# A hybrid state-space and attention block on one core: units moved in the schedule, GELU in place, tied queue order and a token-major end

## The chip, the core and the metric

The kernel runs on one NeuronCore of a Trainium2 chip. The metric is the device time of one execution in microseconds, the median of several runs. The engines are TensorE (PE, whose weight loads are listed apart as PEld), VectorE (DVE), ScalarE (ACT) and GpSimd (POOL); SyncE (SP) issues most of the transfers. Each works through its own queue in order and waits for the others through semaphores.

## The reference

One layer is computed in float32 for 2048 tokens of width 1024:

```
h      = rmsnorm(x);  proj = h @ w_in            # u (512), q, k, v (512 each)
y_ssm  = complex diagonal state-space scan of u (32 groups of 16, 64 states each) + d*u
y_ssm  = gelu(y_ssm);  y_ssm *= sigmoid(y_ssm @ w_glu + b_glu)
y_att  = attention, 8 heads of 64, chunks of 64 frames that see themselves and 8 chunks back,
         with a learned bias by clipped relative distance
x      = x + [rmsnorm(y_ssm), rmsnorm(y_att)] @ w_out
x      = x + (silu(h2 @ w_gate) * (h2 @ w_up)) @ w_down      # h2 = rmsnorm(x), width 2816
out    = rmsnorm(x)
```

## The kernel before

Most products are made three times over: each operand is split into a high part (a cast on ACT) and the rest (a subtraction on DVE), `split` at L151, and `mm3` at L145 issues high by high, high by low and low by high. The kernel is built with a scheduler that puts each engine's instructions in order by priority (about that of the program text) and by its own estimate of when they are ready; it may therefore put an instruction ahead of one that the text has first. PE's instructions of the stages spoken of here are kept in the order of the text.

The work runs in stages. The first 127 us make u and the constants of the state-space part. Then comes the attention stage, `att_phase` (L694), from about 127 to 703 us: 128 steps (four blocks of 512 tokens, four pairs of heads, two heads, four query tiles of 128), and in each step `scores` (one PSUM buffer `sc`, added to the bias and reduced to its least value by DVE at L881, then the exponential on ACT at L884), `transp` for the step two before (five transposes into one PSUM buffer `pt`, copied out by ACT at L899 and by DVE at L900), every fourth step `pv_head`, and then the units.

A unit (`Unit`, L672) is a generator with a first and a last step; `advance(s)` draws so many of its parts that it ends in time. Units are the projections of queries and keys (`qk_unit`, L761) and of values (`v_unit`, L814) at the steps of `CUT`, the scaled and split inputs of the next block (`hT_unit`, L731) at `HTA` and `HTS`, and the eight pairs of `ssm_front` (L568, a product on PE, then a scan of some 100 small operations on POOL) and `ssm_back` (L643, two products for each group, whose result is written to the scratch tensor y). `SX` and `SY` (L669, L670) are their first steps: fronts at 4, 24, 35, 48 and so on to 100, backs at 20, 36 and so on to 114. The second front loads its input into a tile U that the first back still uses. A unit's `pre` says how many steps ahead its loads are issued, all on SP's one queue.

At step 119 (`OPEN`) the generator `mix_phase` (L1001) is opened. Its first `MIX_N` = 26 parts run beside the last steps: y comes in (`fetch`), the weights of the gate (GLU) are split, a GELU of 128x2048 is made for the first 512 tokens (`load`, L1055), eight empty parts (`PY`), the 16 parts of the first block's gate (`glu`, L1078), then `load` for the second block. After the attention stage the second gate, the split of `w_out` and the normed inputs `m` follow (to about 731 us), then the products with `w_out`, gate and up (to about 1782 us) and `down_phase` (L1514). Its last part takes 1024 tokens in pieces of 512, 256 and 256 (`TAIL`): eight tiles of 128 features each, transposed (features on the partitions), the squares summed by products with ones, the root by 14 DVE operations (`newton`, L98), spread over the partitions by transposes (`spread`, `rstd_steps`, L126), multiplied and written out in eight transfers.

Of the kernel before, what the change touches and what calls it, by code (L numbers as in the profile page):

```python
# [9 lines left out]
F32 = mybir.dt.float32  # L10
# [25 lines left out]
OPEN, GSTART = 119, 122  # L36
R1 = 13
SGB = 2
RA1, RA2 = 2, 12
# [3 lines left out]
HTP = 2  # L43
PRO = 0, 0, 2, 2, 2, 2, 0, 0, 0
# [10 lines left out]
TAIL = (0, 512), (512, 256), (768, 256)  # L55
# [26 lines left out]
class K:  # L82
    def __init__(self, tc, io):
        self.tc, self.nc, self.io = tc, tc.nc, io
        self.n = 0
        self.te = Ordered(tc)
        self.ta = self.te if PINA else tc.nc.tensor
# [25 lines left out]

def tok_sums(k, te, ps, c, sq):

    for i in range(4):
        te.matmul(ps[:, c + i : c + i + 1], sq[:, i * P : (i + 1) * P], k.ones[:], start=True, stop=True)
# [8 lines left out]
def rstd_steps(k, te, psum, pool, tag, sq, n, out, nt=None, **kw):  # L126
# [4 lines left out]
    for i in range(nt):  # L131
        for m, sq in enumerate(sqs):
            te.matmul(ps[:, i : i + 1], sq[:, i * P : (i + 1) * P], k.ones[:], start=m == 0, stop=m == len(sqs) - 1)
    with k.tc.high_priority():
        o = newton(k, pool, ps[:, :nt], n, nt)
# [432 lines left out]
def ssm_front(k, p, psum, S, b, eng):  # L568
# [8 lines left out]
    U = S["rsn"][:, : GB * NC].rearrange("p (g c) -> p g c", g=GB) if b and b % 2 == 0 else k.t(p, "U", [P, GB, NC])[:]  # L577
    k.U[b] = U
    load(U.rearrange("p g t -> p (g t)"), S["u"].rearrange("j (c g) n t -> (j c) (g n t)", c=CH)[:, GB * NC * b : GB * NC * (b + 1)])
# [5 lines left out]
    for q in range(GP):  # L585
        ps = k.t(psum, "pj", [P, 2, NC], bufs=2)
        for g2 in range(2):
            k.ta.matmul(ps[:, g2, :], bst[:, 2 * q + g2, :], U[:, 2 * q + g2, :], start=True, stop=True)
# [54 lines left out]
def ssm_back(k, p, psum, S, b):  # L643
# [4 lines left out]
    nc.sync.dma_start(tm[:], S["tm"][:, gs])  # L648
    vm = k.t(p, "Vm", [P, GB, P])
# [18 lines left out]
SX = 4, 24, 35, 48, 61, 74, 87, 100  # L668
SY = 20, 36, 49, 62, 75, 88, 101, 114  # L669


class Unit:  # L672


    def __init__(self, gen, n, s0, s1, pre=0, done=0, light=1, mid=None):
# [3 lines left out]
    def advance(self, s):  # L679
# [3 lines left out]
        want = 1 if self.mid is None or s < self.s0 - self.mid else 2  # L683
# [10 lines left out]
def att_phase(k, ident, S, aw, x0, roots):  # L694

    tc, nc, io, pfs = k.tc, k.nc, k.io, k.pfs
    with ExitStack() as cx:
        hT, vts, qk, keep = {0: tuple(zip(*x0))}, {}, {}, {}

# [5 lines left out]
        def load_ws(sb, ns):  # L705
# [4 lines left out]
            for i, n in enumerate(ns):  # L710
# [5 lines left out]
                elif raws:  # L716
                    with tc.high_priority(offset=-WAY):
# [13 lines left out]
        def hT_unit(sb, q0=0, q1=KT):  # L731
# [13 lines left out]
            else:  # L745
                load(q0)
                for q in range(q0 + 1, q1, 2):
                    load(q, 2)
            for q in range(q0, q1):
# [3 lines left out]
                xt = xts[q]  # L753
                for v, n in zip(hT[sb], ("hi", "lo")):
                    v.append(k.t(aw, f"{n}{q}x" if q < DB and sb % 2 else f"{n}{q}", [P, SB], F32R)[:])
                nc.vector.scalar_tensor_tensor(xt, xt, k.gm[:, q : q + 1], S["rsn"][:, ts], op0=ALU.mult, op1=ALU.mult)
                nc.scalar.copy(hi[q], xt)
                nc.vector.tensor_tensor(lo[q], xt, f32(hi[q]), op=ALU.subtract)
            yield

        def qk_unit(sb, pr):  # L761
# [13 lines left out]
            for c in range(2):  # L775
                if c == 0 or not both:
                    cc = range(2) if both else (c,)
                    pss += [k.t(pfs, "pf", [P, 512]) for _ in cc]
                    for q in range(KT):
                        cs = slice(q * P, (q + 1) * P)  # L780
                        for m in cc:
                            wh, wl = ws[m]
                            mm3(k.ta, pss[m][:], wh[:, cs], wl[:, cs], hi[q], lo[q], q == 0, q == KT - 1)
                            if q == 2:
                                keep_w(4 * m + pr)
                        if q < KT - 1:
                            yield
                ps = pss[c]
                if sb == 0:
                    t = k.t(aa, "yt", [P, SB]) if pr else k.t(aw, "xt", [P, SB], bufs=XB)  # L790
                    nc.vector.tensor_tensor(t[:], ps[:], S["rsn"][:, :SB], op=ALU.mult)
                    ps = t
                for hh in range(2):
                    q2h, q2l, k2 = ts[hh]
                    a = slice(hh * 64, hh * 64 + 64)
                    o = slice(64 - hh * 64, 128 - hh * 64)
                    if c == 0:
                        ways = (a, o) if both and hh == 0 else (a,)
                        for w in ways:
                            nc.scalar.activation(q2h[w, :], ps[a, :], AF.Copy, scale=-0.125)  # L800
                            nc.vector.scalar_tensor_tensor(q2l[w, :], ps[a, :], -0.125, f32(q2h[a, :]), op0=ALU.mult, op1=ALU.subtract)
                        if len(ways) == 1:
                            nc.sync.dma_start(f32(q2h[o, :]), f32(q2h[a, :]))
                            nc.sync.dma_start(f32(q2l[o, :]), f32(q2l[a, :]))
                    else:
                        nc.scalar.copy(k2[a, -SB:], ps[a, :])
                        nc.vector.tensor_tensor(k2[o, -SB:], ps[a, :], f32(k2[a, -SB:]), op=ALU.subtract)
                        if sb < NSB - 1:
                            nc.sync.dma_start(S["k"][sb % 2, 2 * pr + hh], f32(k2[:, -SB:]))
# [4 lines left out]
        def v_unit(sb, fh):  # L814
# [5 lines left out]
            for i in range(4):  # L820
# [15 lines left out]
                if sb == 0:  # L836
                    r = roots()[:, i : i + 1]
                    nc.scalar.activation(vt[:, :, :HD], pv3, AF.Copy, scale=r)
                    nc.vector.scalar_tensor_tensor(vt[:, :, HD:], pv3, r, f32(vt[:, :, :HD]), op0=ALU.mult, op1=ALU.subtract)
                else:  # L840
                    nc.scalar.copy(vt[:, :, :HD], pv3)
                    nc.vector.tensor_tensor(vt[:, :, HD:], pv3, f32(vt[:, :, :HD]), op=ALU.subtract)
# [12 lines left out]
        def scores(st):  # L855
# [25 lines left out]
            nc.vector.tensor_tensor_reduce(  # L881
# [865 lines left out]
```

## Time and profile before

| | |
|---|---|
| median of three runs | 2242.87 us (2241.45 to 2247.27) |
| the profiled execution | 2241.38 us, of which the span in the trace is 2239.6 us |
| mean granted TensorE clock | 0.988 |
| busy PE, DVE, ACT, POOL | 2153.6, 1543.1, 1004.6, 354.1 us |
| bytes moved | 430.16 MB, 192 GB/s on average |

The profile is of one execution. A line of a view names the kernel's line, the engine, the operation and the tiles (written <- read); a bracket at the end of a timeline row gives the idle time of the engine just before it and what ended that. In a view of windows each engine has its busy time in the stretch, and PEclk is the clock that PE was granted (1.00 is full speed).

### The profile page before, as it was taken

To read this page: it belongs to the slowest core of one execution; us is meant where nothing else is said; L and a number is where in the kernel's file an instruction comes from. 1 tells how busy PE (TensorE), PEld (TensorE's weight loads), DVE (VectorE), ACT (ScalarE), POOL (GpSimd) and SP (SyncE) were. 2 spreads that over 40 slices of the span, in tenths; PEclk is the share of its full clock that TensorE was granted. 3 is DMA by queue.
4 is the path that set the end of the run, shared out by engine and by line. 5 is a ranking of instruction groups with operands and counts; after the bars stand their busy time and mean duration, and the time that the engine had idled before them with its cause. 6 is when DMAs were issued, how large, how long until landed. Compare 5 with 4: busy or idle time off the path is not lost.

```text
span 2239.6 us, 30165 instructions
## 1 busy us (share of the span) xinstructions
PE 2153.6 (96%) x10632; PEld 1819.1 (81%) x10632; DVE 1543.1 (69%) x2706; ACT 1004.6 (45%) x1667; POOL 354.1 (16%) x830
## 2 busy tenths in 40 slices
PE   8988898999988999999999999999999999999997
PEld 6777797999977788788888887888888788888886
DVE  8756767555557666767766768767665577688776
ACT  6355565556567541443333335333333343353322
POOL 3354666666600000000000000000000100000000
PEclk9999999999999999999999999999999999999999
DMA  9778867666552436835645557546333495465642
GB/s 330 231 249 283 270 207 229 193 196 193 179 175 99 137 116 206 275 118 173 198 153 200 198 191 258 199 160 207 108 115 97 136 371 198 159 226 183 217 174 76
DMA packets 194664, 430.16 MB, mean 192 GB/s; under 512 B 19792, under 2 KB 38272, under 8 KB 187408
## 3 DMA queue, kind: packets, MB, share of 16 engines
q1 hardware_dynamic: 186768, 403.26, 54.3%
q0 software_dynamic: 7744, 24.97, 3.6%
q8 instruction: 83, 1.36, 0.3%
q14 instruction: 69, 0.57, 0.1%
HBM read 288.95 MB, written 131.10 MB: 188 GB/s over the span
## 4 chain that ended last, share of the span: by engine, by line
PE 81%; DMA 7%; DVE 6%; ACT 2%; issue 2%; SPq 1%; DVEq 0%; ACTq 0%
PE X L76 20%; PE ps L76 18%; PE pf L76 11%; PE Y L76 10%; PE big L76 7%; PE W L76 5%; PE pj L76 4%; PE pt L79 2%; PE sc L76 2%; DMA acc<-x 1%; DMA hd<-wc 1%; DMA x<-xt 1%; DMA lo<-hc 1%; DMA w<-wss 1%; DVE ptl L900 0%
## 5 line engine op out<-in xcount | busy, mean ns | idle before, releaser
L76 PE MATMUL X<-hi,c 128*128 128x512 f32 x1408 | 450.9, 391 | 6.5 <-DVE c L153 3.4
L76 PE MATMUL ps<-hd,hd 128*128 128x512 f32 (+1 forms) x1968 | 428.1, 379 | 3.3 <-DVE hd L153 2.0
L76 PEld LDWEIGHTS ps<-hd,hd 128*128 128x128 f32 x1968 | 356.4, 188 | 73.6 <-DVE hd L153 2.7
L76 PEld LDWEIGHTS X<-hi,c 128*128 128x128 f32 x1408 | 264.9, 188 | 63.6 <-DVE c L153 4.5
L76 PE MATMUL X<-lo,c 128*128 128x512 f32 x704 | 274.7, 390 | 0.0
L153 ACT CAST hd<-hd 128x1536 fp32r<-128x1536 f32 (+1 forms) x106 | 147.5, 1394 | 231.0 <-DMA hd<-hq 174.6
L76 PE MATMUL Y<-hi,c 128*128 128x512 f32 x704 | 225.2, 390 | 2.4 <-DVE u L1428 2.4
L153 DVE TENSOR_TENSOR hd<-hd 128x1536 fp32r<-128x1536 f32 (+1 forms) x106 | 174.1, 1644 | 38.6 <-ACT hd L153 38.3
L1532 POOL DMA_DIRECT2D hd<-hq x7 | 5.3, 757 | 1165.3 <-PE X L76 1151.2
L153 DVE TENSOR_TENSOR c<-S,c 128x512 fp32r<-128x512 f32 x176 | 120.9, 688 | 99.3 <-ACT c L153 99.0
L1424 ACT COPY u<-X 128x512 f32<-128x512 f32 x132 | 77.5, 588 | 197.4 <-PE X L76 197.3
L153 ACT CAST c<-S 128x512 fp32r<-128x512 f32 x176 | 109.4, 622 | 120.8 <-PE Y L76 61.8
L76 PE MATMUL big<-m,woh 128*128 128x512 f32 x512 | 161.5, 397 | 0.0
L76 PEld LDWEIGHTS Y<-hi,c 128*128 128x128 f32 x704 | 132.6, 188 | 31.0 <-DVE u L1428 3.2
L1566 DVE TENSOR_TENSOR acc<-acc,ps 128x512 f32<-128x512 f32 x196 | 130.1, 682 | 37.9 <-PE ps L76 37.7
L76 PEld LDWEIGHTS X<-lo,c 128*128 128x128 f32 x704 | 132.7, 188 | 27.4
L153 ACT CAST c<-raw 128x512 fp32r<-128x512 f32 x132 | 82.2, 623 | 150.2 <-PE Y L76 73.0
L76 PE MATMUL pf<-hi,w 128*128 128x512 f32 x416 | 148.7, 409 | 0.0
L76 PE MATMUL Y<-lo,c 128*128 128x512 f32 x352 | 137.2, 390 | 0.0
L900 DVE TENSOR_TENSOR ptl<-pt,pth 128x640 fp32r<-128x640 f32 (+3 forms) x152 | 98.3, 647 | 54.6 <-ACT pth L899 53.1
L884 ACT ACTIVATE s<-s,mn 128x640 f32<-128x640 f32 (+4 forms) x128 | 97.9, 765 | 61.9 <-DVE mn L881 58.6
L899 ACT CAST pth<-pt 128x640 fp32r<-128x640 f32 (+3 forms) x152 | 83.7, 551 | 83.2 <-PE pt L79 78.8
(451 smaller groups left out, 4269.1 us busy)
## 6 DMA issues: line engine op xcount, KB each, us to landing
w<-wss SPq DMA_DIRECT2D x36, 1024.0 KB, 6.2
hq<-g SPq DMA_DIRECT2D x140, 256.0 KB, 2.1
hd<-hq SPq DMA_DIRECT2D x35, 768.0 KB, 4.4
hd<-wc SPq DMA_DIRECT2D x35, 768.0 KB, 5.8
raw<-in_w_gate SPq DMA_DIRECT2D x44, 512.0 KB, 3.7
raw<-in_w_up SPq DMA_DIRECT2D x44, 512.0 KB, 4.1
wc<-px SPq DMA_DIRECT2D x66, 256.0 KB, 3.1
wss<-w SPq DMA_DIRECT2D x12, 1024.0 KB, 6.1
```

Source lines behind the costliest of these rows:

```text
L76: return self.tc.keep_in_program_order(self.tc.nc.tensor.matmul(*a, **b))
L79: return self.tc.keep_in_program_order(self.tc.nc.tensor.transpose(*a, **b))
L153: return nc.scalar.copy(hi, raw), nc.vector.tensor_tensor(lo, raw, f32(hi), op=ALU.subtract)
L884: nc.scalar.activation(s[:, :nk], s[:, :nk], AF.Exp, bias=mn[:], scale=-1.0, accum_out=sums[sb, pr][:, hh, qp : qp + 1])
L899: nc.scalar.copy(pth[:, a:b, qp, :], pt[:, a:b, :])
L900: nc.vector.tensor_tensor(ptl[:, a:b, qp, :], pt[:, a:b, :], f32(pth[:, a:b, qp, :]), op=ALU.subtract)
L1424: nc.scalar.copy(u[:], ps[:])
L1532: (nc.gpsimd if aside else nc.sync).dma_start(f32(lo), src.rearrange("g p c -> p g c"))
L1566: V.tensor_tensor(a, a, ps[:], op=ALU.add)
```

## The change

It has five parts.

1. **State-space units sooner.** `SX` and `SY` become 4, 19, 33, 45, 56, 68, 80, 92 and 20, 34, 46, 57, 69, 81, 93, 105. The second front (b == 1) loads its input in two halves into the tiles hi0x and lo0x, which the first pair of heads has left, and the second back loads it again into U. All loads but the first front's come four steps ahead.
2. **Inputs of a block.** For the third and fourth block the units of `hT_unit` move from 12 to 6 steps ahead of the block to 26 to 8 ahead; the last five tiles are scaled first and split all at step -9. In the last pair of each block the keys' product takes tiles 3 to 7 first. The value weights of the first block (units 9 and 11) are loaded six steps ahead, not four, and split in two parts.
3. **Order on DVE.** `k.least` is the latest reduction of `scores`. Instructions under `behind()` get an edge that keeps them after it on DVE: the copies out of PSUM of queries, keys and values, the scaling, the splits named above and the gate's splits.
4. **GELU.** At step 108 (`FETCH`) the state-space pool is given back, and y of the first 1024 tokens and half of the gate's weights are loaded. GELU runs in place in four pieces of 128x1024 at steps 111, 113, 115, 117, pinned in ACT's order. `take` then only rearranges each block, eight copies of 128x512 on POOL. `GSTART` is 120 (was 122), and `MIX_N` 21 parts.
5. **The end.** `TAIL` keeps (0, 512) and (512, 256). The last 256 tokens are made token-major (`by_tokens`): tokens on the partitions, 512 features in a PSUM bank, the residual added by products with the identity, the squares summed by ACT's accumulator, the root from ACT's Sqrt and four DVE operations (`root`, `refine`), and the gain taken from a row that one transfer spreads over the partitions. They go to an output of their own, out_t. The sums of the two pieces before use `root` as well.

```diff
-OPEN, GSTART = 119, 122
+FETCH, GELU, OPEN, GSTART = 108, (111, 113, 115, 117), 119, 120
...
-RA1, RA2 = 2, 12
+RA0, RA1, RA2 = 3, 10, 14
...
+HTE, HTM, HTL = (-26, -20), -10, (-9, -8)
...
+def root(k, pool, ps, n, w):
...
+    k.nc.scalar.activation(o[:], ps, AF.Sqrt, scale=1.0 / n, bias=k.eps)
+    V.tensor_scalar(v[:], ps, -0.5 / n, -0.5 * EPS, op0=ALU.mult, op1=ALU.add)
+    return refine(V, v, f, y, o)
...
+    V.reciprocal(y[:], o[:])
+    V.tensor_tensor(f[:], y[:], y[:], op=ALU.mult)
+    V.tensor_tensor(f[:], f[:], v[:], op=ALU.mult)
+    V.scalar_tensor_tensor(o[:], f[:], 1.5, y[:], op0=ALU.add, op1=ALU.mult)
...
+    if b == 1:
+        us = [lent(q).rearrange("p (g c) -> p g c", g=2) for q in range(GP)]
+        for q in range(GP):
+            load(us[q], ssm_input(S, b, slice(q, q + 1)))
...
+    if b == 1:
+        k.U[b] = k.t(p, "U", [P, GB, NC])[:]
+        nc.sync.dma_start(k.U[b], ssm_input(S, b))
...
-SX = 4, 24, 35, 48, 61, 74, 87, 100
-SY = 20, 36, 49, 62, 75, 88, 101, 114
+SX = 4, 19, 33, 45, 56, 68, 80, 92
+SY = 20, 34, 46, 57, 69, 81, 93, 105
...
+        def behind(on=True):
+            return tc.issue_after(k.least) if on and k.least else nullcontext()
...
-                    with tc.high_priority(offset=-WAY):
+                    if n == 11:
+                        yield
+                    with tc.high_priority(offset=-WAY), behind(ns == (9, 11)):
...
+            ahead = q0 and sb > 1
+            if ahead:
+                for q in range(q0, q1):
+                    yield
+                    scaled(q)
...
+                with behind(ahead):
+                    nc.vector.tensor_tensor(lo[q], xts[q], f32(hi[q]), op=ALU.subtract)
...
+                    qs = [*range(DB, KT), *range(DB)] if c and pr == 3 else range(KT)
...
+                with behind():
+                    for hh in range(2):
...
+            k.least = ins.ins
...
+            if s == FETCH:
+                sp.release()
+                k.my0 = tc.alloc_tile_pool(name="my0", reuse_waits="tile", bufs=1)
+                k.y0 = k.t(k.my0, "y0", [P, 4, L, 128])
+                for f in range(4):
+                    nc.sync.dma_start(k.y0[:, f], S["y"][:, f * P : (f + 1) * P, :128].rearrange("j p t -> p j t"))
+                k.wg = k.t(k.my0, "wg", [P, 2, DS])
+                nc.sync.dma_start(k.wg[:], io["w_glu"][: 2 * P].rearrange("(q p) n -> p q n", p=P))
...
+                    if s in GELU:
+                        y = k.y0[:, GELU.index(s)]
+                        tc.keep_in_program_order(nc.scalar.activation(y, y, AF.Gelu_apprx_tanh))
...
+                if sb < 2:
+                    nc.gpsimd.tensor_copy(yo, yv[:, f].rearrange("p j c -> p c j"))
...
+        def by_tokens(t0, hs, ds, acc):
...
+            for c in range(2):
+                for n, ((hh, hl), (dh, dl)) in enumerate(zip(hs, ds)):
+                    mm3(te, ps[c][:], hh[:, 0, ts], hl[:, 0, ts], dh[:, 0, c * 512 : c * 512 + 512], dl[:, 0, c * 512 : c * 512 + 512], n == 0, n == len(hs) - 1, skip_group_check=True)
+                    if n == 0:
+                        for i in range(4):
+                            te.matmul(ps[c][:, i * P : (i + 1) * P], acc[4 * c + i][:, ts], k.ident[:], start=False, stop=False, skip_group_check=True)
...
+                    nc.scalar.activation(j[:], ps[c][:], AF.Square, accum_out=sq[c][:])
...
+                nc.scalar.activation(o[:], sq[1][:], AF.Sqrt, scale=1.0 / D, bias=f[:])
+                V.tensor_scalar(v[:], sq[1][:], -0.5 / D, y[:], op0=ALU.mult, op1=ALU.add)
+                refine(V, v, f, y, o)
+                nc.scalar.activation(ta, ta, AF.Copy, scale=o[:])
+                V.scalar_tensor_tensor(b[:], ps[1][:], o[:], g[:, 512:], op0=ALU.mult, op1=ALU.mult)
...
+        for n, _ in enumerate(chain.from_iterable(by_tokens(t0, hs, ds, acc) for t0 in TOKENS)):
+            if n == 2:
+                last.sums(root=root)
+            if n == 5:
+                last.products()
```

249 lines of the change are left out of this document (153 added, 96 removed).

## The prediction

> **What bounds the kernel now.** The first part of the page comes first, then the stretches of the span, the list of who waited for whom, and the timelines of the places found.
>
> ```profile
> span 2239.6 us, 30165 instructions
> ...
> PE 2153.6 (96%) x10632; PEld 1819.1 (81%) x10632; DVE 1543.1 (69%) x2706; ACT 1004.6 (45%) x1667; POOL 354.1 (16%) x830
> ```
>
> PE is busy 96% of the span, so 2239.6 - 2153.6 = 86 us of idle PE is all there is to win, unless PE's work itself becomes less or faster. Gate, up and down, where most of the time lies, keep PE full and are not touched. The question is which of the idle places the change reaches. Waits of PE in the attention stage, from 120 to 260 us and from 260 to 400 us (total, count, longest), and from 640 to 735 us:
>
> ```profile
> PE sc L76 <- DVE mn L881: 5.7, 1, 5.7
> PE pj L76 <- DMA Bst<-bsts: 2.6, 1, 2.6
> PE sc L76 <- issue: 2.2, 1, 2.2
> ...
> PE pt L79 <- DVE ptl L900: 4.5, 2, 3.1
> PE sc L76 <- DVE k L807: 4.1, 1, 4.1
> ...
> PE pt L79 <- DVE ptl L900: 14.1, 3, 6.6
> ```
>
> An idle PE also costs afterwards. These windows lie right behind the longer waits:
>
> ```profile
> 183.00:188.40 5.40, 4.97 (x23) 5.00 (x24) 1.56 (x7) 1.72 (x6) 4.77 (x14) 0.50 1.01 379
> 370.00:372.60 2.60, 2.60 (x10) 2.36 (x11) 2.13 (x4) 1.16 (x3) 2.50 (x4) 0.50 0.45 183
> 668.70:671.10 2.40, 2.37 (x9) 1.96 (x9) 2.40 (x5) 2.40 (x6) 0.00 (x0) 0.50 0.93 298
> 676.80:681.20 4.40, 4.35 (x15) 3.58 (x15) 0.00 (x0) 4.39 (x2) 0.00 (x0) 0.60 0.00 0
> ```
>
> PE is granted half the clock there (0.50, third number from the end), so busy time times the missing share of the clock is lost as well: 4.97 x 0.50 = 2.5, then 1.3, 1.2 and 4.35 x 0.40 = 1.7 us.
>
> **The attention stage.** Step 12 waits 5.7 us, and 2.5 us go by the clock. The chain of waits and DVE's timeline say for what:
>
> ```profile
> 175.32 4.51 DMA nbb<-nbs
> ...
> 180.53 2.54 DVE L153 TENSOR_TENSOR w<-raw,w 128x512 fp32r<-128x512 f32 x4
> ```
>
> The bias nbb was issued behind the value weights and landed at 179.8; then four splits of these weights (2.54 us) ran ahead of the step's reduction. The weights are now loaded two steps sooner and the splits held behind a reduction. The splits leave the path, the bias lands a little earlier, and the clock stays up if the wait is short: 5 us, between 0 and 8.2.
>
> The second front's loads stood on SP behind the first back's store; with the input in other tiles, loaded at step 15 and not 22, the 2.6 us for Bst go. Moved along are two input loads and Bst (step 15) and a second load of U (512 KB, step 28), behind which SP's small loads have two steps of slack. The 2.2 us before step 24 are keys copied out just before use, whose steps stay. Gain 2.6, between 0 and 4.8. The later fronts and backs move 2 to 9 steps; their products move from one full stretch of PE to another, which costs nothing, and POOL's 354.1 us are at most 44 for each of eight fronts, which stand 11 to 15 steps of some 4 us apart, so a back seldom waits for its scan.
>
> Steps 35 and 56 wait because inputs of a later block were put ahead of copies that PE needs:
>
> ```profile
> 271.14 2.14 DVE L756 SCALAR_TENSOR_TENSOR raw<-raw,g_mix,rsn 128x512 f32<-128x512 f32 x1
> ...
> 362.96 0.82 DVE L881 CUSTOM_DVE_ANT_0 s<-sc,nbb 128x640 f32<-128x640 f32 x1
> ...
> 363.71 0.70 DVE L758 TENSOR_TENSOR lo<-raw,hi 128x512 fp32r<-128x512 f32 x1
> ...
> 366.17 2.99 DVE L758 TENSOR_TENSOR lo<-raw,hi 128x512 fp32r<-128x512 f32 x2
> ```
>
> The scaling is now held behind the step's reduction and the block's inputs come earlier. I take 2.5 of the 3.1 us at step 35 (0 to 3.1). At step 56 and shortly behind it 4.1 + 1.4 us of waiting (4.5 - 3.1 leaves 1.4) and 1.3 us of clock are at stake, but five tiles are split at once in step 55: 5 x 0.70 = 3.5 us of DVE may again stand before a reduction. I take 3.5 of 6.8 (0 to 6.8), and 1 us lost at step 87, which did not wait before (0 to 3.5).
>
> What is late next is DVE beside POOL. The operations above took 2.14 us and about 1.5 us instead of 0.70 while POOL worked on a scan. The second front now scans beside the 16 such operations of the second block, in steps 20 to 26. How much PE loses to this is nowhere alone in the trace; the nearest stretch with both, inputs and scan, is
>
> ```profile
> 364.00:392.00 28.00, 22.15 (x114) 18.52 (x113) 25.19 (x36) 14.63 (x29) 12.99 (x13) 0.94 0.76 230
> ```
>
> where all causes together left PE idle 28.00 - 22.15 = 5.9 us. I take 2 of 0 to 5.9, nearer the low end since DVE is otherwise less full there. The Trainium skill (SBUF — State Buffer, section "SBUF: two separate sides") says that VectorE and GpSimd share a port pair that one holds for a whole instruction, also against a VectorE operation with two SBUF inputs; the slow rows agree. By that rule each of the 16 could wait for a whole POOL instruction.
>
> GELU's price on ACT:
>
> ```profile
> 671.68 1.28 ACT L884 ACT_TABLE_LOAD   x1
> 672.98 0.83 ACT L884 ACTIVATE s<-s,mn 128x640 f32<-128x640 f32 x1
> ...
> 677.63 3.79 ACT L1065 ACTIVATE ys<-yr 128x2048 f32<-128x2048 f32 x1
> ...
> 702.99 1.92 ACT L1094 ACTIVATE yr<-yr 128x2048 f32<-128x2048 f32 x1
> ...
> 617.00:648.00 31.00, 31.00 (x200) 28.59 (x199) 14.51 (x27) 14.64 (x29) 0.00 (x0) 1.00 0.46 138
> ```
>
> A piece of 128x1024 costs half of 1.92 (in place) to half of 3.79 (rearranged), so 1.0 to 1.9; I take 1.0, the row in place. With a table load before and one for the next exponential that is 1.28 + 1.0 + 1.28 = 3.6 us, four times 14.2. The last window covers those steps: ACT 14.6 us of 31. The sum, 28.8 (32.4 at the dear end), just fits, and transposes lag two steps behind their scores, which hides one piece. I count a loss of 2 us, between 0 and 5. On SP the five loads of step 108 (2.5 MB) stand before those of step 110; the like fetch of y took 6.5 us, and the first piece comes three steps later, so they are hidden.
>
> Attention stage: 5 + 2.6 + 2.5 + 3.5 - 1 - 2 - 2 = 8.6, about **9 us**.
>
> **From attention to the products with w_out.** Windows up to the end of the first gate and on to the start of w_out:
>
> ```profile
> 653.50 6.54 DMA yr<-y
> ...
> 650.00:698.00 48.00, 31.23 (x173) 26.28 (x172) 29.21 (x63) 37.36 (x53) 0.00 (x0) 0.86 0.40 121
> 698.00:731.00 33.00, 29.61 (x143) 23.65 (x141) 32.29 (x58) 24.69 (x32) 0.00 (x0) 1.00 0.49 165
> ```
>
> In the first, PE idles 48.00 - 31.23 = 16.8 us and loses 1.2 + 1.7 = 2.9 by the clock: the fetch of y and the two GELUs of 3.79 stand on ACT between the casts that release `pt`. All of that is now done before. PE then needs 48 - 19.7 = 28 us. But DVE has 29.2 us of work in this window, the gate's splits included, and none of it moves out; so the floor is DVE's, a gain of 18.8 at most. Queues that wait on each other don't pack fully: at 85% DVE needs 34.4 us, a gain of 13.6. The eight POOL copies have no row. By the nearest,
>
> ```profile
> L617 POOL TENSOR_TENSOR X<-X,fx 128x434 f32<-128x434 f32 x32 | 35.7, 1116 | 2.1
> ...
> L605 POOL TENSOR_TENSOR st<-X,a 128x128 f32<-128x128 f32 x56 | 28.7, 513 | 160.7 <-ACT X L591 156.9
> ```
>
> each costs 0.5 to 1.1 us; I take 1.1, the size nearer 512. Only the first is waited for, the rest hides behind steps 119 to 122, but they run beside splits with two inputs. I take **13 us**, between 5 and 19. In the second window DVE is busy 32.3 of 33 us and keeps its work: no gain.
>
> **The end.**
>
> ```profile
> 1848.36 268.69 PE ps L76 x1192
> ...
> 2184.69 0.63 ACT L1596 ACTIVATE sa<-acc 128x512 f32<-128x512 f32 x1 [11.64 <-DVE acc L1582]
> ...
> 2202.33 0.98 PEld L76 LDWEIGHTS ps<-ones,sa 128*128 128x128 f32 x8
> ...
> 2207.59 0.65 PE L79 MATMUL ps<-ident,no 128*128 128x128 f32 x4 [1.21 <-DVE no L110]
> 2207.99 8.88 PE L76 MATMUL ps<-hd,hd 128*128 128x256 f32 x72
> ...
> 2222.03 0.43 PE L79 MATMUL ps<-ident,no 128*128 128x128 f32 x2 [1.40 <-DVE no L110]
> 2222.21 3.12 PE L76 MATMUL ps<-hd,hd 128*128 128x256 f32 x24
> ...
> 2231.31 0.16 DVE L110 SCALAR_TENSOR_TENSOR no<-nf,ny 128x2 f32<-128x2 f32 x1
> ...
> 2232.32 3.22 DVE L1612 SCALAR_TENSOR_TENSOR acc<-acc,g_final,ps 128x256 f32<-128x256 f32 x8 [0.85 <-PE ps L79]
> ...
> 2209.67 27.29 SPq L1613 DMA_DIRECT2D out<-acc  x24
> ...
> 172.63 0.46 SPq L803 DMA_DIRECT2D q2h<-q2h  x1
> ```
>
> The last products end at 2222.21 + 3.12 = 2225.3, and 14.3 us follow: sums, 14 root operations, a spread, eight products, eight stores. In the new form PE does 2 x 24 products of 512 columns at 268.69 / 1192 = 0.225 us, 10.8 us, in place of 96 of 256 at 8.88 / 72 = 0.123, 11.8 us, and 16 identity products in full float32. The four such products of the sums show as eight records in 0.98 us, 0.245 each, 3.9 us for 16; the transposes (four in 0.65 with their end, 0.11 to 0.16 each) would make it 1.8. I take 3.9, the same kind of product: PE does 2.9 us more. The waits of 1.21 and 1.40 go, since the shorter root is done while more products run. So the products end at 2225.6. Behind them come the square (0.63 and reading its sum, 0.8), the square root and four small DVE operations (0.2 each, 1.0), the last product (0.7), two issues (0.46 each by the last row, as 27.29 / 24 is mostly waiting), and the 2.6 us from SP's last issue (2209.67 + 27.29 = 2236.96) to the end of the span: 6.0 us in place of 14.3. Gain 8.3 - 0.3 = 8, of which I take **7.5**, between 4 and 9. The gain row's load (512 KB) and the Sqrt table are fetched ahead, beside full PE; on the path the table would cost 1.28. The second piece's eight products (3.22 us) and eight stores fall beside the last tile.
>
> **Sum.** 9 + 13 + 7.5 = 29.5 us. The profiled execution took 2241.38, which gives 2211.9; it lay 1.5 us under the median of 2242.87, so I forecast 2213 for the median.
>
> **Rivals.** (a) *DVE and ACT become the bound*: steps 119 to 130 run at DVE's pace with slow splits (gain 5, not 13), and the GELU steps lose 5, not 2. 2213 + 8 + 3 = 2224. For it: 29.2 us of DVE work against 28 of PE; against: the lag of two steps. The Trainium skill (ScalarE: Activation LUTs, "What ACT_TABLE_LOAD costs") speaks for it: a switch costs a drain of 1380 ns beside the load of 1283 ns. Eight switches would then take some 21 us, by estimate. The rows above show the exponential 0.02 us behind its table load and no drain, so I give that little weight.
> (b) *All stalls go and the clock stays up*: 8.2 + 2.6 + 3.1 + 6.8 = 20.7 in the attention stage, less 4 for the new costs, then 19 and 9: 45, 2198. For it: each has its edit; against: the 2.2 us before step 24 and DVE's load.
> (c) *The attention stage doesn't gain*: waits only move, as each is the last of several; with rival (a)'s gain of 5 and 7.5 at the end, 12.5 us: 2230.
> (d) *Slower*: `behind` decides. If copies out of PSUM are ready before the step's reduction, each waits for it, 0.82 us of a reduction at full width. That counts from the point where PE waits for the bank that the copy frees. Each block has 8 groups of copies for queries and keys and 8 for values, 64 in all: 52 us, 2213 + 52 = 2265. Against it: the scores stand before the projections on PE in each step, so the reduction is ready first.
>
> **Chances.** Forecast 0.58 (own range 2203 to 2221), (a) 0.17, (b) 0.13, (c) 0.07, (d) 0.05. The range is 2198 to 2227: it leaves out (c), (d) and a part of (b). About 0.3%, 7 us, is what a measurement of this kernel can tell from no change: faster than 2236 0.92, within 0.04, slower 0.04.
>
> **What would show it.** In the changed profile: no 5.7 us wait of `sc` at step 12, none for Bst, none of 3 us at steps 35 and 56; GELU rows of about 1.0 us between two table loads, with ACT under 31 us in those steps; PE idle under 5 us between the last projection and the second gate; two rows of the last store within 7 us of the last product. Wrong would be a PE full of waits below 1 us for DVE in all steps (rival d), or DVE splits of 1.5 us beside POOL copies (rival a).

## The result, and the profile after

The changed kernel takes 2223.76 us (median of six executions, 2217.26 to 2226.85) where the kernel before took 2243.26 beside it (six, 2241.45 to 2247.41): 19.5 us less by these medians, whose quotient is 0.9913. The ratio given with the result, 0.9896 with a 95% interval of 0.9883 to 0.9909, is 23 us; it is not the quotient of the medians, and in the table below the two differ by up to 0.0017. The forecast was 2213, in a range of 2198 to 2227. The profiled execution took 2217.26, the shortest of the six, with a mean granted clock of 0.992; the five others show 0.988 to 0.990. Its span is 24.5 us shorter than that of the kernel before.

The first part of the page of after: engines, busy time, share of the span.

```profile
span 2215.1 us, 30093 instructions
PE 2153.9 (97%) x10606; PEld 1817.4 (82%) x10606; DVE 1534.0 (69%) x2671; ACT 1009.9 (46%) x1681; POOL 372.8 (17%) x838
```

PE's busy time is the same as before (2153.6). All of the gain is PE's idle time: 2215.1 - 2153.9 = 61.2 us of it, where there were 86.

Now both kernels by stage. The stretches are cut at the same instructions: the reductions of step 0, step 119 and step 127, the first spread among the products with w_out (some of them stand ahead of it), the start of the last tiles, the end. In each row: length, PE, PEld, DVE, ACT and POOL busy (count), granted clock, DMA share, GB/s. First before, then after:

```profile
128.85:651.51 522.66, 497.51 (x3058) 448.82 (x3057) 310.59 (x599) 292.93 (x632) 296.18 (x730) 0.99 0.68 213
651.51:693.11 41.60, 25.22 (x138) 21.57 (x139) 25.60 (x57) 33.37 (x46) 0.00 (x0) 0.84 0.46 140
693.11:731.00 37.89, 34.34 (x167) 27.33 (x165) 35.21 (x64) 27.90 (x37) 0.00 (x0) 1.00 0.42 144
731.00:1848.36 1117.36, 1103.69 (x4888) 911.34 (x4889) 769.02 (x1265) 445.39 (x709) 10.45 (x14) 0.99 0.54 181
1848.36:2239.60 391.24, 376.07 (x1772) 315.40 (x1772) 300.28 (x424) 136.89 (x128) 0.00 (x0) 0.99 0.51 176
```

```profile
128.39:644.77 516.38, 496.61 (x3058) 446.00 (x3057) 307.10 (x598) 307.86 (x645) 306.51 (x732) 0.99 0.71 220
644.77:677.35 32.58, 27.95 (x146) 24.02 (x147) 25.77 (x47) 20.25 (x39) 8.26 (x7) 0.84 0.32 114
677.35:715.94 38.59, 33.56 (x159) 27.36 (x157) 36.34 (x73) 27.47 (x37) 0.00 (x0) 0.96 0.40 140
715.94:1831.60 1115.66, 1102.01 (x4888) 910.34 (x4889) 769.28 (x1265) 447.46 (x711) 10.45 (x14) 1.00 0.54 182
1831.60:2215.10 383.50, 377.07 (x1746) 315.01 (x1746) 293.12 (x388) 138.68 (x134) 0.00 (x0) 1.00 0.52 180
```

The attention stage gained 522.66 - 516.38 = 6.3 us (9 forecast), the transition, which is the second and third row, 9.0 - 0.7 = 8.3 (13 forecast), the end 7.7 (7.5 forecast). The long middle, which the change does not touch, is 1.7 shorter, and the start 0.5. Together 24.5.

Where the attention stage still waits. The list of who waited for whom (total, count, longest) from 120 to 260, 260 to 400 and 400 to 645 us:

```profile
PE pt L82 <- DVE ptl L955: 4.8, 7, 1.0
...
PE sc L79 <- DVE mn L935: 3.3, 2, 2.8
PE sc L79 <- issue: 2.2, 1, 2.2
...
PE sc L79 <- DVE k L860: 1.3, 1, 1.3
...
PE pt L82 <- DVE ptl L955: 3.0, 2, 2.7
PE sc L79 <- DVE k L860: 2.3, 1, 2.3
```

Step 12 waits 2.8 us instead of 5.7; the wait for Bst is gone; the 3.1 of step 35 is gone; step 56 waits 1.3 instead of 4.1. Two long waits are new: 2.3 us for a key in step 88 and 2.7 us for a transpose in step 112, behind the first piece of GELU. The lines left out from 120 to 260 us are short but for one of 4.2 us, which lies ahead of step 0 and is the same in the kernel before. The timeline around the first piece (start, us, engine, instruction):

```profile
610.36 1.28 ACT L1058 ACT_TABLE_LOAD   x1
...
611.65 1.06 ACT L1058 ACTIVATE y<-y 128x1024 f32<-128x1024 f32 x1
...
612.99 1.28 ACT L938 ACT_TABLE_LOAD   x1
...
614.28 0.83 ACT L938 ACTIVATE s<-s,mn 128x640 f32<-128x640 f32 x1
...
615.11 0.67 ACT L954 CAST pth<-pt 128x640 fp32r<-128x640 f32 x1
...
616.78 0.74 PE L82 MATMUL pt<-ident,s 128*128 128x128 f32 x5 [2.69 <-DVE ptl L955]
```

The transposes that this cast (615.11) releases were done at 611.4; it stands on ACT behind both table loads, the piece between them and an exponential.

The end, from the second last identity products to the last store:

```profile
2205.55 1.05 PE L79 MATMUL ps<-ident,acc 128*128 128x128 f32 x8
...
2206.36 2.32 PE L79 MATMUL ps<-hd,hd 128*128 128x512 f32 x9
...
2208.71 0.60 ACT L1720 ACTIVATE sg<-ps 128x512 f32<-128x512 f32 x1 [2.97 <-PE ps L79]
...
2210.60 0.75 DVE L1731 SCALAR_TENSOR_TENSOR ob<-ps,no,rsn 128x512 f32<-128x512 f32 x1
2211.28 0.33 SPq L1733 DMA_DIRECT2D out_t<-rsn  x1
2211.72 0.38 SPq L1734 DMA_DIRECT2D out_t<-ob  x1
```

The last product ends at 2206.36 + 2.32 = 2208.7 and the span 6.4 us later (14.3 us in the kernel before). Four identity products are eight records in 1.05 us, so 4.2 us for 16.

### The profile page after: what moved, and what is told of

It reads as the page before. It is cut to its first block, busy times and chain, and to the rows that moved or that the text cites. A ratio compares the mean times of both kernels' runs of the same rounds, so it can differ in the third digit from the quotient of the medians.

```text
span 2215.1 us, 30093 instructions
## 1 busy us (share of the span) xinstructions
PE 2153.9 (97%) x10606; PEld 1817.4 (82%) x10606; DVE 1534.0 (69%) x2671; ACT 1009.9 (46%) x1681; POOL 372.8 (17%) x838
## 4 chain that ended last, share of the span: by engine, by line
PE 82%; DVE 8%; DMA 6%; issue 3%; ACT 2%; SPq 0%; POOL 0%; ACTq 0%; DVEq 0%
PE X L79 20%; PE ps L79 19%; PE pf L79 10%; PE Y L79 10%; PE big L79 6%; PE W L79 5%; PE pj L79 5%; PE pt L82 2%; PE sc L79 2%; DMA lo<-hc 1%; DMA hd<-wc 1%; DMA x<-xt 1%; DVE lo L175 1%; DMA xt<-in_xt 1%; DVE ptl L955 1%
```

## The experiments

**Theory:** each part does what it says, and the sizes are off: waits of steps 12, 88 and 112 remain or are new, the transition keeps its idle time because DVE and ACT are full there and DVE is slowed by POOL, and half of the difference from execution to execution is TensorE's clock. **Rivals:** the order behind the reductions costs (d); ACT or DVE is the bound (a); the gain is lost in stages that are not touched.

All ratios are to the kernel before on the same chip: 2243.26 us for after, 2244.62 for tail_only to gelu_one, 2243.10 for again to copy_act, 2244.64 for the last four. The last two columns say how many us sooner than in before the reduction of step 116 and the first spread among the products with w_out start ("w_out begins" below), counted from the reduction of step 0 in the profiled execution. By step 116 all state-space units are done in both orders. These columns are of one execution each, and chance moves them: up to step 108 the programs of after, again, gelu_one, lo_pool, copy_act and gstart are the same, and there they stand between 5.7 and 8.1 us ahead of before.

| kernel | median us | ratio, 95% interval | step 116 | w_out |
|---|---|---|---|---|
| after | 2223.76 | 0.9896, 0.9883 to 0.9909 | 6.3 | 14.6 |
| tail_only | 2233.89 | 0.9959, 0.9943 to 0.9976 | -0.6 | -0.5 |
| ssm_only | 2239.55 | 0.9980, 0.9967 to 0.9993 | 0.5 | 0.5 |
| no_behind | 2228.90 | 0.9935, 0.9918 to 0.9952 | -1.5 | 6.9 |
| gelu_one | 2220.31 | 0.9886, 0.9864 to 0.9909 | 11.5 | 20.8 |
| again | 2222.25 | 0.9913, 0.9898 to 0.9928 | 5.6 | 15.2 |
| mid31 | 2221.97 | 0.9904, 0.9889 to 0.9919 | 9.0 | 18.1 |
| front2 | 2249.02 | 1.0020, 1.0009 to 1.0032 | -17.4 | -9.9 |
| copy_act | 2228.75 | 0.9933, 0.9918 to 0.9948 | 5.6 | 9.7 |
| gstart | 2224.88 | 0.9912, 0.9895 to 0.9929 | 4.7 | 11.7 |
| lo_pool | 2219.92 | 0.9891, 0.9873 to 0.9908 | 6.8 | 15.0 |
| both | 2214.70 | 0.9869, 0.9851 to 0.9888 | 12.4 | 22.0 |
| ht_old | 2226.39 | 0.9921, 0.9907 to 0.9936 | -0.3 | 8.0 |

**tail_only**: the kernel before with part 5 alone.

```diff
-TAIL = (0, 512), (512, 256), (768, 256)
+TAIL = (0, 512), (512, 256)
+TOKENS = 768, 896
...
```

> The kernel before with the token-major end alone (part 5). Theory: the end's gain is its own and adds to the rest, 7.7 us as the two traces show (6.4 us after the last product instead of 14.3, products 0.1 later): 2243.3 - 7.7 = 2235.6, 0.9966 of before; the span up to the last tile is unchanged. Rival (the part of the gain that the medians miss, 24 us in the profiled executions against 19.5, is lost in the end or in the stages that the change does not touch, for instance by the gain row's load beside the down products): 2238 to 2241, with the start of the last tiles later than before's.

The ratio lies 0.0041 under 1, which is 9.2 us, with an interval of 5.4 to 12.8 that holds the theory's 7.7. The stretch of the end as a window:

```profile
1850.57:2237.00 386.43, 379.93 (x1746) 317.07 (x1746) 292.74 (x388) 138.62 (x134) 0.00 (x0) 0.99 0.51 177
```

It takes 386.43 us, after 383.50. PE is idle for 6.5 us of it and for 6.4 in after; the rest is PE's busy time at a lower clock. The end is an independent gain.

**ssm_only**: the kernel before with `SX`, `SY`, `lent` and the second load of U.

> The kernel before with the state-space units begun sooner and the second input in the dead tiles (parts 1 and 2 without the inputs of a block), GELU and the rest as before. Theory: the wait for Bst (2.6 us, step 24) goes, and waits of PE of 1 to 3 us in sum come in steps 20 to 27 because the second block's input operations stand on DVE beside the second front: 2242 to 2244, 1.000 of before, the gain at step 26 within 1 us of nothing; later fronts and backs cost nothing. Rival (moving the units is a gain by itself, the 3 us of small waits are the work of the ordering behind the reductions, not of the second front): 2239 to 2241, no small waits in steps 20 to 27.

The time speaks for the rival (1.6 to 7.4 us less by the interval), the trace for the theory: at step 116 only 0.5 us are won. What the expectation lacked is in the waits from 400 to 640 us:

```profile
PE sc L76 <- DVE k L820: 3.1, 1, 3.1
```

There the kernel before waits for nothing over 0.2 us. So the new wait of step 88 comes with the moved units: a front's scan on POOL now stands beside the splits of the fourth block's inputs (two of them took 2.16 us), and the key is split behind them. The wait of 3.1 us at step 35 is gone in ssm_only too; two of 0.8 and 0.9 us stand at step 36. Up to step 116 PE is idle for 22.1 us where before has 24.9, but at a granted clock of 0.50 for 20.7 us where before has 15.6. Whether the 4.5 us of the ratio are more than clock stays open.

**no_behind**: after with the edges on DVE left out, those of the gate's splits too.

```diff
-            return tc.issue_after(k.least) if on and k.least else nullcontext()
+            return nullcontext()
...
-            with tc.issue_after(k.least):
+            with nullcontext():
```

> After without the order on VectorE (no instruction is held behind a reduction, the gate's splits included). Theory: the order gains little by itself because loads and units also moved: at step 12 PE waits 2.8 to 5.7 us (now 2.8), at step 35 and 56 up to 3 us come back, and the waits of 1 to 2.7 us in steps 88 and 112 stay; 2223.8 + 2 to 8 = 2226 to 2232. Rival (d), the order is what costs (instructions queued behind a held one are late): 2216 to 2221, with fewer waits below 1 us on DVE in all steps.

The waits from 120 to 260 and from 260 to 400 us:

```profile
PE sc L79 <- DVE mn L935: 6.0, 2, 5.0
...
PE sc L79 <- DVE k L860: 4.5, 1, 4.5
...
PE pt L82 <- DVE ptl L955: 1.5, 1, 1.5
```

Step 12 waits 5.0 us again, step 56 waits 4.5 and step 35 waits 1.5. The theory holds and rival (d) falls: at step 116 the kernel stands 7.8 us behind after and 7.1 behind again. Of the 7.8, 5.7 are PE's idle time up to there (25.2 us against 19.6).

**ht_old**: after with the inputs of blocks 3 and 4 (2 and 3 in the expectation, which counts from 0) in their old place. The last five tiles are scaled and split one by one again, and their splits are not held behind a reduction.

```diff
-            ahead = q0 and sb > 1
+            ahead = False
...
-                a, b = HTA if sb == 1 else HTE
+                a, b = HTA
...
```

> After with the inputs of blocks 2 and 3 in their old place (twelve to six steps ahead of the block, scaled and split one by one), the scaling still held behind a reduction. Theory: the wait of 2.3 us in step 88 goes (before had none) and step 56 waits 3 to 4 us again instead of 1.25, with up to 2 us at step 35 or 87: between after - 1 and after + 3, 2222 to 2226. Rival 1 (the new place is the gain of steps 35 and 56): 2227 to 2230. Rival 2 (the order behind reductions alone gains it, the new place costs): 2219 to 2221.

The waits from 260 to 400 and from 400 to 640 us:

```profile
PE sc L79 <- DVE k L860: 1.3, 1, 1.3
PE pt L82 <- DVE ptl L955: 0.9, 1, 0.9
...
PE pf L79 <- DVE lo L808: 3.6, 1, 3.6
PE pt L82 <- DVE ptl L955: 2.7, 1, 2.7
PE sc L79 <- DVE k L860: 1.3, 1, 1.3
```

The expectation was wrong in its places. Step 56 waits 1.3 as in after, so it is the order and not the earlier place that helps there. The fourth block is worse: 1.3 and 3.6 instead of 2.3. The place, with the order of those splits, is worth 6.6 us at step 116, of which 2.9 are PE's idle time and the rest is clock, and 2 to 6 us by the ratios (0.9921 against 0.9913 and 0.9896). Against again the intervals overlap.

**mid31**: after with the last value weight's splits one step later.

```diff
-                    pre, mid = (6, (3, 2)) if c == 4 else (4, (2,))
+                    pre, mid = (6, (3, 1)) if c == 4 else (4, (2,))
```

> After with the splits of the last value weight one step later, behind the reduction of step 12 (their two instructions stand ahead of it now). Theory: at step 12 three splits (1.98 us, ending at 179.77) still stand between the landing of the bias (177.77) and the reduction; with two of them behind it, PE's wait of 2.8 us falls to 1.0 to 1.6, and 1 to 2 us of that are left at step 116: 2222 beside 2223.8. Rival (the bias and the casts set it, the splits only fill the time): the wait stays between 2.5 and 2.9 and the time is that of after.

DVE around step 12 in after, and then the wait in mid31:

```profile
177.79 1.98 DVE L175 TENSOR_TENSOR w<-raw,w 128x512 fp32r<-128x512 f32 x3
179.69 0.28 DVE L935 CUSTOM_DVE_ANT_0 s<-sc,nbb 128x128 f32<-128x128 f32 x1
```

```profile
PE sc L79 <- DVE mn L935: 1.8, 2, 1.5
```

The wait fell from 2.8 to 1.5 as expected. In after all four splits run between the reductions of steps 11 (171.84) and 12 (179.69), three of them behind the landing of the bias: the edge held the last two behind the former reduction, one step too early. The medians, 2221.97 and 2223.76, do not tell the two kernels apart.

**front2**: after with the second front at step 24 again and the units between shifted. The edit turns the second front's own branches off, so its input goes into the tile U as in before; the "own tile" of the expectation is not what ran.

```diff
-    if b == 1:
+    if b < 0:
...
-SX = 4, 19, 33, 45, 56, 68, 80, 92
-SY = 20, 34, 46, 57, 69, 81, 93, 105
+SX = 4, 24, 36, 47, 58, 69, 80, 92
+SY = 20, 35, 47, 58, 69, 80, 92, 105
...
```

> After with the second front begun at step 24 as before (own tile for the input, loaded at step 22) and the units between moved accordingly; GELU, order and end as in after. Theory: the second front beside the inputs of the second block costs some 3 us of small waits (steps 20 to 27), which go, and the wait for Bst (2.6 us) returns: the step-28 reduction stands 4 to 6 us ahead of before's less the work that has not yet been done, and at step 64 the kernel is within 1.5 us of after; 2222 to 2226. Rival 1 (the second front sooner is the gain of this part): 2227 to 2229. Rival 2 (it is a loss): 2219 to 2221.

At step 28 all these kernels have issued the same products (576). There front2 stands 1.0 us ahead of before, and the six kernels with the second front at step 19 (after, again, gelu_one, lo_pool, copy_act, gstart) 2.4 to 4.7. So the sooner second front is not the loss of rival 2. Whether its 1 to 4 us are more than clock stays open: PE's idle time up to there is 11.6 us in front2, 11.7 in after and 10.4 in again (14.1 in before). The rest of the expectation missed. The waits from 260 to 600 us:

```profile
PE pj L79 <- DMA XG<-X: 8.7, 3, 3.6
PE pj L79 <- issue: 4.3, 2, 3.7
```

Five times a back's products wait on PE for what the scan leaves (XG). These backs follow their fronts by 11 or 12 steps; in after it is 12 to 16, and none of its backs waits.

**gelu_one**: after with one GELU of 128x4096 in step 117.

```diff
-                    if s in GELU:
-                        y = k.y0[:, GELU.index(s)]
+                    if s == GELU[-1]:
+                        y = k.y0[:]
```

> After with the four pieces of GELU as one instruction of 128x4096 in step 117, in place: three pairs of table loads fewer (3 x 2 x 1.28 = 7.7 us of ScalarE). Theory: the pieces cost PE only the 2.7 us in step 112 and ScalarE is not the bound between; one run of 1.28 + 4.2 + 1.28 = 6.8 us in step 117 is longer than the lag of two steps hides by some 1 to 4 us, so 2222 to 2226. Rival (a), ScalarE is the bound of steps 111 to 118 by its table loads: 2216 to 2220, with PE full in step 117.

The piece on ACT's timeline:

```profile
631.15 1.28 ACT L1058 ACT_TABLE_LOAD   x1
632.45 3.63 ACT L1058 ACTIVATE y<-y 128x4096 f32<-128x4096 f32 x1
636.09 1.28 ACT L938 ACT_TABLE_LOAD   x1
```

These 6.2 us in one go cost PE one wait of 2.0 at step 118; four pieces cost 2.7 at step 112. Between step 108 and w_out gelu_one gains 3.9 us on after and 4.2 on again; another 2.2 of the table's difference to after lie ahead of step 108, where the edit does not reach. The median lies between the two expectations, nearer the rival's.

**copy_act**: after with the copies of `take` on ACT.

```diff
-                    nc.gpsimd.tensor_copy(yo, yv[:, f].rearrange("p j c -> p c j"))
+                    nc.scalar.copy(yo, yv[:, f].rearrange("p j c -> p c j"))
```

> After with the eight copies of GELU's result on ScalarE instead of GpSimd. Theory (rival (a) of the prediction, in part): splits of the gate take 0.83 to 1.56 us beside GpSimd's copies instead of 0.68; without them they take 0.68 to 0.70 all, DVE is free 2 us sooner, PE's waits in steps 119 to 121 (4.7 us in all) fall by 1 to 2 us and w_out begins 1 to 3 us sooner: 2221 to 2223. Rival (ScalarE is as full there, so eight copies of 0.6 us ahead of the casts that release the transposes cost as much): waits of PE for pth or ptl grow, w_out begins 1 to 4 us later, 2224 to 2228.

**lo_pool**: after with eight of the gate's subtractions on POOL.

```diff
...
-            split(k, gh[:], gl[:], b.ys[f])
+            nc.scalar.copy(gh[:], b.ys[f])
+            (nc.gpsimd if b in (b0, nxt) else nc.vector).tensor_tensor(gl[:], b.ys[f], f32(gh[:]), op=ALU.subtract)
...
```

> After with the eight low-part subtractions of the first two gate blocks on GpSimd instead of VectorE (0.68 us each there, 5.4 us in all). Theory (VectorE's work is the bound of the transition): w_out begins 2 to 5 us sooner, 2218 to 2222. Rival (GpSimd beside VectorE's operations with two SBUF inputs costs as much as it takes off, and GpSimd at 1.1 to 1.5 us each is the longer queue behind its copies): VectorE's splits of the weights stay at 0.8 to 1.6 us, PE waits for gl, w_out begins 1 to 6 us later, 2224 to 2229.

Splits of gate weights on DVE (count: least, median, greatest ns) in after, then with the copies on ACT, then with subtractions on POOL too:

```profile
L175 DVE TENSOR_TENSOR wgl<-sg,wgh x2: 677/1118/1559, 652.0 to 655.6; 128x512 fp32r<-128x512 f32 x2
```

```profile
L175 DVE TENSOR_TENSOR wgl<-sg,wgh x2: 681/684/686, 659.1 to 661.4; 128x512 fp32r<-128x512 f32 x2
```

```profile
L175 DVE TENSOR_TENSOR wgl<-sg,wgh x2: 1331/1444/1558, 649.3 to 652.3; 128x512 fp32r<-128x512 f32 x2
```

POOL's copies do slow these splits. But copy_act loses 5 us to w_out, more than its rival's 1 to 4, since eight copies of 1.07 us (0.6 taken) stand on ACT ahead of the casts that release `pt`. Its waits from 645 to 720 us:

```profile
PE pt L82 <- DVE ptl L955: 9.6, 3, 7.5
```

And lo_pool begins w_out within 0.4 us of after, though its median, 2219.92, lies in the range of the theory. Its DVE is busy 59.3 us in the transition and that of after 62.1, so the eight subtractions that went left only 2.8 us less: the splits of the weights grew beside them. The length stayed, 71.3 and 71.2 us. So DVE's work is not shown to set the length of the transition. That the contention alone sets it is not shown either, since copy_act takes it away and fills ACT in its place.

**gstart**: after with the gate from step 122 on.

```diff
-FETCH, GELU, OPEN, GSTART = 108, (111, 113, 115, 117), 119, 120
+FETCH, GELU, OPEN, GSTART = 108, (111, 113, 115, 117), 119, 122
```

> After with the gate's second and later parts from step 122 on (as before) instead of 120; GpSimd's copies and the first splits still come at step 119. Theory (the transition is held up because the gate's twelve splits, the last keys and the copies meet in steps 119 to 121): the waits of 4.7 us in sum at 645 to 655 become 2 to 3, the clock drop there (4.4 us lost) shortens, but the gate then lies behind the attention stage: w_out begins between 1 us sooner and 3 us later; 2222 to 2226 beside after's 2223. Rival (steps 119 to 121 are not where the transition is lost, the length of the gate's chain is): w_out begins 3 to 6 us later, 2226 to 2229.

w_out begins 3 us later, at the edge of both expectations; the time, 2224.88, is in the range of the theory and not to be told from that of after and again.

**again**: after, unchanged.

> After, unchanged, for a second trace beside its variants. Theory: what the executions differ by is TensorE's granted clock after short waits, not the waits: PE's idle time in the attention stage agrees with the first trace within 1 us, and the time follows the mean clock (first six: 2217.3 at 0.992, 2222 to 2227 at 0.988 to 0.990, some 2.4 us for each 0.001); median 2222 to 2226. Rival (the first trace was fast because waits were shorter): idle time differs by 3 us or more.

The waits in the attention stage are nearly the same (19.5 us of idle PE up to step 119, 19.8 in after), and w_out begins 0.6 us sooner. Then the two executions part. The middle stretch of again:

```profile
715.41:1841.55 1126.14, 1108.18 (x4888) 914.48 (x4889) 770.26 (x1265) 446.40 (x711) 10.45 (x14) 0.99 0.54 180
```

It takes 10.5 us more than in after for the same 4888 products: 6.2 of PE's busy time, by the clock, and 4.3 of idle time. The theory holds for the attention stage; behind it waits differ too, by more than the rival's 3 us.

**both**: gelu_one and mid31 in one kernel.

> The two edits that each took waits away, in one kernel: GELU's four pieces as one in step 117, and the last value weight's splits one step later. Theory: they lie in different places and add, so the reduction of step 116 stands 13 to 15 us ahead of before's and w_out begins 8 to 9 us sooner than in after; without luck of the clock 2216 to 2219. Rival (the clock gives it back): as gelu_one or mid31 alone, 2220 to 2222.

The median of 2214.70 is the shortest of all: 0.0131 under before, 29 us (25 to 33). It is below the expected 2216 to 2219, while step 116 (12.4, 13 to 15 expected) and w_out (7.4 us sooner than in after, 8 to 9 expected) fell short. The two edits add: gelu_one gained 3.9 behind step 108 and mid31 3.5 in all.

## Why the prediction was right or wrong

The direction and the range were right; the order of the parts was not (transition, attention, end at 13, 9 and 7.5 us; measured 8.3, 6.3 and 7.7, in again 9.6, 5.6 and 6.1). The median of 2223.76 lies outside the forecast's own 2203 to 2221 and at rival (a)'s 2224. That agreement is luck, since (a) had 5 us for the transition and a loss of 5 for GELU, where 8.3 and 2.7 were measured.

The profiled execution was to be 2211.9 and was 2217.3: 2.7 us were missing in the attention stage and 4.7 in the transition, 2.4 more than forecast came from the middle, the start and the end, and 0.4 went outside the span. The other 5.4 us of the miss of 10.8 are the step from the profiled execution to the median: it was taken as in before, 1.5 us, of which the round 2213 kept 1.1, and is 6.5, where this execution had the highest clock of the six.

- **Step 12 (5 forecast).** The wait shrank by 2.9. "The splits leave the path" is the step that failed: the bias landed at 177.8, 2 us sooner, but three splits still stood between it and the reduction. mid31 takes 1.3 us more. The clock, which was part of the 5, is chance: behind this wait of 2.8 us it stayed at 1.00 in after and fell to 0.50 for 6.8 us in again, so that between steps 11 and 14 after gains 4.8 us and again 2.7.
- **Bst and the second front (+2.6 and -2).** The wait for Bst went, and short waits of 2.7 us in all came in steps 19 to 25 of after, 1.6 in again. So the sum of 0.6 is -0.1 in after and 1.0 in again by the waits; by front2 at step 28 it is 1 to 4, most of it clock.
- **Later fronts "cost nothing".** Wrong: ssm_only has the new wait at the fourth block (3.1 us) from this part alone. After waits 2.3 there, where 1 was forecast. No back waits for its scan in after, as forecast, but the reason given, the distance between fronts, is not enough: front2 shows that 11 steps from a front to its back are too few.
- **Steps 35 and 56 (2.5 and 3.5).** Right: 3.1 and 2.8 us of waiting went. At step 56 the cause is the order (4.5 us in no_behind), not the earlier inputs (1.3 in ht_old). At step 35 the order has half of it (1.5 in no_behind); ssm_only loses the wait of 3.1 without the order.
- **GELU (-2).** The piece is 1.06 us, ACT is busy 28.4 of the 32 us from 609 to 641 (28.8 of 31 forecast), and PE loses 2.7. "Transposes lag two steps behind their scores, which hides one piece" failed: the cast that frees `pt` stands on ACT behind the piece and the exponential that it delayed. With one piece instead of four, 3.9 us are won by w_out.
- **Transition (13 forecast, 8.3).** The floor by DVE's work with 85% packing is the step that failed. From step 119 to step 127 DVE is busy 25.8 of 32.6 us (79%), and with 2.8 us less of its work in lo_pool the transition is no shorter. By the windows, PE's idle time fell from 16.4 + 3.6 to 4.6 + 5.0 us, 10.3 less. But the same 305 products took 2.0 us longer (27.95 + 33.56 against 25.22 + 34.34), at a clock of 0.84 and 0.96 where it was 0.84 and 1.00: the 2.9 us of clock that were to come back did not. In again they came in part: the clock was 0.95 and 1.00, the products took 58.0 us (59.6 in before), PE was idle for 11.8 us, and the gain was 9.6. The copies on POOL were dearer than taken (1.07 to 1.58 us, 1.1 taken). My reading is that PE, ACT and DVE hand one tile on to the next there and that each experiment moved the delay to a neighbour. That is argued, and what would shorten the chain itself stays open.
- **End (7.5 forecast, 7.7).** Right in each term within 0.4 us: 6.4 us follow the last product where 6.0 were forecast, and an identity product takes 0.26 where 0.245 was taken.
- **The rivals.** (d) is refuted: without the order the kernel loses 5 to 9 us (0.9935 against 0.9913 and 0.9896; 4 to 5 by the quotients of the medians). Of (a), the transition came out between its 5 and the forecast's 13, and its DVE rows of 1.56 us are there, but lo_pool does not bear out its cause. (b) and (c) did not come. The Trainium skill (ScalarE: Activation LUTs, "What ACT_TABLE_LOAD costs") has a drain of 1380 ns at each switch; the rows of after show none: piece and exponential each begin 0.01 us behind their table load.

## What to carry to other kernels

A VectorE instruction without hurry should be ordered behind the one that TensorE waits for in the same step; which step it is tied to matters as much as the tie. A short table-switching operation costs where it delays a buffer's release, so one long run at a quiet place can be cheaper than four short ones. A forecast of an execution time should not count on clock that is to "come back", and should add the spread of the clock to its range. Positions of two kernels should be compared only where both have issued the same products.

## What the runs showed of the hardware

TensorE's clock falls in pieces of one size, and not in proportion to a wait. Behind nearly every place the granted clock is 0.50 for 3.4 us or a small multiple of it, which costs 1.7 us a piece where PE is busy, after a wait of 4.2 us as after one of 0.25. The same instructions can escape it. These rows hold the sums of one block of w_out, with products of one column and 0.25 us of idle PE just ahead, in after and in before:

```profile
785.00:789.40 4.40, 4.15 (x30) 3.69 (x29) 2.59 (x6) 1.22 (x2) 0.00 (x0) 0.99 0.23 84
789.40:792.80 3.40, 3.40 (x10) 2.62 (x9) 3.40 (x19) 1.69 (x2) 0.00 (x0) 0.51 0.61 206
```

```profile
803.00:807.60 4.60, 4.35 (x31) 3.85 (x30) 2.54 (x6) 1.22 (x2) 0.00 (x0) 1.00 0.24 90
807.60:811.00 3.40, 3.40 (x17) 2.79 (x16) 3.40 (x19) 1.68 (x2) 0.00 (x0) 1.00 0.60 215
```

In after 10 products pass in 3.4 us, in before 17. Likewise the wait of 3.4 us at the first gate product (it ends at 1364.40 in after and at 1368.48 in again) left the clock at 1.00 in after and at 0.50 for 6.8 us in again:

```profile
1364.00:1368.00 4.00, 3.60 (x16) 2.97 (x17) 3.35 (x6) 0.98 (x2) 0.00 (x0) 1.00 0.24 62
```

```profile
1368.40:1371.60 3.20, 3.12 (x7) 2.49 (x8) 3.04 (x6) 0.00 (x0) 0.00 (x0) 0.50 0.17 20
1371.60:1374.80 3.20, 3.20 (x9) 2.49 (x8) 1.03 (x2) 1.10 (x2) 0.00 (x0) 0.51 0.86 289
```

The clock records of the traces show what decides: where a wait falls on a fixed grid. In each of the 14 traces all drops begin a whole number of steps of 3.413 us apart (in after at 127.17, 226.15 and 506.05 us, the latter two 29 and 111 steps behind the first). Cut into such windows from the first drop on, the 14 traces have 78 at full clock in which PE was busy for less than 1.4 us; a drop follows every one. Of those with more than 2.0 us a drop follows only 28, and each of these holds products of one column. The wait at the first gate product lies in one window in again (PE busy for 0.54 us of it) and across two in after (1.58 and 1.81 us). The one-column products of after above lie in one window, 785.94 to 789.35, and those of before across two.

The Trainium skill (TensorE: Matmul & The Clock Gate, "Part 1: The HAM clock gate (the "warmup" mystery)") says that activity is watched in windows of 3413 ns that run freely. The grid agrees. It also names an idle window of some 3.4 us as what closes the gate; here a window with PE busy for up to 1.4 us was enough, or 0.25 us of idle time beside one-column products, so the measurement decides.

A GELU of 128x4096 in place took 3.63 us and four of 128x1024 took 4.24; with the table loads that is 6.2 against 14.5 us of ScalarE.
